# First stage of a two-block network on one NeuronCore: the input rows requested first, the first quarter of the modulation as TensorE matmuls

## The chip, the cores and the metric

One core of a Trainium2 chip runs one program. The metric is the device time of a run in microseconds. The engines that matter are TensorE (PE in the profile, its weight loads PEld), VectorE (DVE), ScalarE (ACT) and the queue on SyncE (SP) that issues every load from memory.

## The reference, cut to what matters

Two blocks, each of depth 2, work on 256 rows of 1024 features. The program's first stage is the opening of the first block's first layer:

```python
cond = jax.nn.silu(c)                       # c: (1, 1024)
mod = cond @ ada_w[l] + ada_b[l]            # ada_w[l]: (1024, 9 * 1024)
sh1, sc1, g1, ... = jnp.split(mod, 9, axis=-1)
hn = _modulate(_rms_norm(h, norm_g[l, 0]), sh1, sc1)   # xn * (1 + scale) + shift
h = h + 0.5 * g1[:, None, :] * _swiglu(hn, ffn1_w_in[l], ffn1_w_out[l])
```

Before the first feed-forward product can begin, the rows of x have to be normed, turned to feature-major form, scaled by `(1 + sc1) * norm_g` and shifted by `sh1`. Scale and shift are products of the vector `cond` with 1024 x 1024 pieces of `ada_w`.

## The kernel before, in words

Every large product runs as three float32r matmuls: operands are split into a high part (`A.copy` with a cast, line 336, ACT) and the rest (`V.tensor_tensor` subtract, line 339, DVE), and `mm3` (lines 368 to 370) adds high x high, high x low and low x high. Weights come as parts of 128 x 1024 floats (512 KB): `load_part` (line 345) takes a raw buffer `wr`, a high buffer `wh` and a low buffer `wl`, and issues the load on SP (line 347). There are three `wr` buffers; one is free again when both halves of the split have read it. A part serves 12 matmuls of 128 x 512: two blocks of 128 features, two row tiles, three products.

The modulation is done on VectorE. `ada_load` (line 678) brings 128 output columns of `ada_w`, laid out one per partition with 1024 inputs along it, and `ada_chunk` (line 683) multiplies them with `cond`, which stands as a copy in every partition, and sums along the partition: one value per partition, a column of `mod`.

`start()` (line 723) is the first stage. It computes the first four of the eleven feed-forward column groups (`FIRST`), and goes through the 1024 features in four pairs of blocks (`p` = 0 to 3, blocks k = 2p and 2p+1). Each pair needs four chunks of the modulation (scale and shift of its two blocks) and four weight parts, and then issues 48 matmuls. Ahead of the pairs stands the row work: `row_rstd` sums squares (line 476, ACT) and takes the reciprocal root (lines 442 to 447), line 740 scales the rows, line 489 transposes them on TensorE against the identity `ident`, which is part of the table `col_sb`, and line 743 copies the result to `xts`. `modulate(k)` (line 747) makes scale and shift out of the two columns of `mod`, applies them on ACT (line 753), casts to `xh` (line 754) and subtracts to `xl` (line 755).

The program is written in the order of the work, and a scheduler of the framework sets each engine's own instruction order at build time. On the chip every engine runs its list strictly in order, and so does SP: a load that waits for a buffer holds up all loads behind it.

```python
for p, pair in enumerate(pairs):
    ...
    for j in range(2):
        for n in pair[2 * j:2 * j + 2]:
            if p or n[1]:
                ada_chunk(0, sum(n), raws.pop(n))
        modulate(2 * p + j)
        for n in range(2 * j, FIRST if j else 2):
            raw, hi, lo = parts[n]
            split(hi, lo, raw)
```

Of the kernel before, what the change touches and what calls it, by code (L numbers as in the profile page):

```python
# [9 lines left out]
F32 = mybir.dt.float32  # L10
F32R = mybir.dt.float32r
BF16 = mybir.dt.bfloat16
# [11 lines left out]
FIRST = 4  # L24
# [156 lines left out]


def pack(inp):
    d = {"ws": pack_weights(inp), "cols": pack_cols(inp), "x": inp["x"].reshape(S, D), "c": inp["c"].reshape(1, D)}
    aw = inp["ada_w"]
    d["adaw"] = aw.reshape(2, D, 72, 128).transpose(0, 2, 3, 1)
    wf = inp["w_in"][:, :, 2560:2564]
    d["wf"] = wf.reshape(2, 8, 128, 4).transpose(2, 0, 1, 3)
    d["gmn"] = np.stack([inp["gmlp_norm_g"], inp["gmlp_norm_b"]], 1).reshape(1, 1024)
    d["wst"] = inp["gmlp_ws"].transpose(3, 0, 1, 2)  # L190
    import ml_dtypes

    def level(b):
        j, t = np.arange(128)[:, None], np.arange(128)[None, :]
        mid = t // (2 * b) * 2 * b + b
        return np.where(t >= mid, (j >= mid) & (j <= t), (j > t) & (j < mid)).astype(np.float32)
# [23 lines left out]
INS = ["ws", "cols", "x", "c", "adaw", "wf", "gmn", "wst", "bmask", "lev", "pred", "sbias", "gains", "lbs"]  # L220


@with_exitstack
def body(ctx, tc, ws, cols, x, c, adaw, wf, gmn, wst, bmask, lev, pred, sbias, gains, lbs, out, phases=range(12)):
    nc = tc.nc
    V, A, T = nc.vector, nc.scalar, nc.tensor
    phases = list(phases)
# [21 lines left out]
    def s2(shape=(128, 512), dt=F32):  # L249
        return s2_p.tile(list(shape), dt, tag="s2", name=nm("s"))  # L250
# [232 lines left out]
    def hh(t, q):  # L483
        return h[:, t, 512 * q:512 * q + 512]
# [183 lines left out]
    const.tile([128, 8], F32, name="trail")  # L668
# [53 lines left out]

    def start():

        pairs = [[(o, k) for k in (2 * p, 2 * p + 1) for o in (8, 0)] for p in range(4)]
# [9 lines left out]
        xts = [s2([128, 2, S]) for _ in range(4)]  # L735
# [8 lines left out]
        acc = [[accum(), accum()] for _ in range(FIRST)]  # L744
        w = [{} for _ in range(FIRST)]

        def modulate(k):
            an_, mod_ = an[0][:, k:k + 1], mod[0][:, k:k + 1]
            A.activation(an_, mod[0][:, 8 + k:9 + k], AF.Identity, scale=C("norm_g", k, 1), bias=g1[:, k:k + 1])
            A.activation(mod_, mod_, AF.Identity, bias=C("ada_b", k, 1))  # L750
# [4 lines left out]
            V.tensor_tensor(out=xl[:, k], in0=xt, in1=xh[:, k].bitcast(F32), op=ALU.subtract)  # L755

        for p, pair in enumerate(pairs):
            half, i = divmod(p, 2)
            parts = []
            for n in pair:  # L760
                if p or n[1]:
                    raws[n] = ada_load(0, sum(n))
            for n in range(FIRST):
                parts.append(load_part(plan["b1", 0, "ffn1", n, half], i))
            for j in range(2):
                for n in pair[2 * j:2 * j + 2]:
                    if p or n[1]:
                        ada_chunk(0, sum(n), raws.pop(n))
# [731 lines left out]
```

## Time and profile before

| | us |
|---|---|
| median of 3 runs | 2214.31 |
| lowest and highest run | 2205.01, 2215.36 |
| the profiled execution | 2208.89 |
| its span in the profile | 2207.1 |
| TensorE busy | 2149.9 (97%) |
| VectorE busy | 1486.1 (67%) |
| ScalarE busy | 1191.5 (54%) |
| loads of 512 KB: weight parts, modulation chunks | 692, 144 |

The profile shows one execution. "Busy" adds the time in which an engine has an instruction under way; matmuls overlap in the pipeline, so the distance between the starts of two of them is less than the duration printed for one. Where a row has "xN" the times are of N instructions merged. A true float32 matmul (not float32r, not a transpose) stands in the trace as two pairs of weight load and matmul: line 944 issues 48 of them in the program, and the trace has 96.

### The profile page before, as it was taken

Reading aid. Unit: us, or ns where it says so; the run is one execution under the profiler, and the core shown is the slowest. Engines: PE = TensorE matmul, PEld = TensorE weight load, DVE = VectorE, ACT = ScalarE, POOL = GpSimd, SP = SyncE. Lnnn points to the kernel's source line nnn. Section 1 sums busy time; section 2 is a strip of 40 time slices with the busy share of each in tenths; the row PEclk is TensorE's granted clock in tenths of the full one; section 3 lists DMA queues with packets and bytes.
Section 4 is the critical chain, followed back from the end, with each engine's and each line's share of the span. In section 5 each row is a group of like instructions: output and inputs, shape, how many; then the busy total and the mean of one; then the engine's idle time right before and its main releaser. Section 6 shows DMA issues by size and latency. Waiting matters only on the chain.

```text
span 2207.1 us, 27771 instructions
## 1 busy us (share of the span) xinstructions
PE 2149.9 (97%) x10148; PEld 1765.8 (80%) x10150; DVE 1486.1 (67%) x2224; ACT 1191.5 (54%) x1933; POOL 0.2 (0%) x4
## 2 busy tenths in 40 slices
PE   6999998999999999999999999999999999999998
PEld 5787776888888777888888888888888887887887
DVE  6788986765888786655754665675566557657653
ACT  6544656544544756553644565464465447556552
POOL 0000000000000000000000000000000000000000
PEclk9999998999999999999999999999999999999999
DMA  8889734885889533755755543475555555245652
GB/s 321 294 318 337 259 118 152 293 265 174 314 336 342 209 113 126 247 181 183 246 187 188 179 143 115 135 234 184 191 181 202 189 171 183 96 143 177 205 182 95
DMA packets 125416, 452.90 MB, mean 205 GB/s; under 512 B 14176, under 2 KB 14432, under 8 KB 125280
## 3 DMA queue, kind: packets, MB, share of 16 engines
q1 hardware_dynamic: 125280, 451.13, 59.2%
q8 instruction: 80, 1.31, 0.2%
q14 instruction: 56, 0.46, 0.1%
HBM read 450.03 MB, written 1.05 MB: 204 GB/s over the span
## 4 chain that ended last, share of the span: by engine, by line
PE 77%; DMA 8%; ACT 7%; DVE 6%; issue 2%; SPq 0%; DVEq 0%; ACTq 0%
PE a L368 23%; PE a L369 22%; PE a L370 22%; DMA wr<-in_ws 8%; ACT wh L336 3%; DVE wl L339 3%; PE t L626 2%; PE t L489 1%; PE t L1234 1%; ACT h L476 1%; DVE spill L683 1%; ACT s L533 1%; PE t L1188 1%; PE t L970 1%; PE t L1346 0%
## 5 line engine op out<-in xcount | busy, mean ns | idle before, releaser
L339 DVE TENSOR_TENSOR wl<-wr,wh 128x1024 fp32r<-128x1024 f32 x692 | 843.2, 1223 | 468.0 <-ACT wh L336 463.0
L336 ACT CAST wh<-wr 128x1024 fp32r<-128x1024 f32 x692 | 726.8, 1052 | 718.5 <-PE a L370 388.1
L368 PE MATMUL a<-wh,xh 128*128 128x512 f32 x1888 | 750.7, 398 | 7.9 <-ACT xh L534 6.0
L369 PE MATMUL a<-wl,xh 128*128 128x512 f32 x1888 | 736.4, 390 | 1.9 <-DVE wl L339 1.9
L370 PE MATMUL a<-wh,xl 128*128 128x512 f32 x1888 | 736.0, 391 | 0.0
L368 PEld LDWEIGHTS a<-wh,xh 128*128 128x128 f32 x1888 | 357.6, 189 | 81.6 <-ACT xh L534 6.7
L370 PEld LDWEIGHTS a<-wh,xl 128*128 128x128 f32 x1888 | 356.9, 189 | 75.5 <-DVE xl L339 1.4
L369 PEld LDWEIGHTS a<-wl,xh 128*128 128x128 f32 x1888 | 357.6, 189 | 73.0 <-DVE wl L339 3.7
L368 PE MATMUL a<-wh,s 128*128 128x512 f32 x896 | 352.2, 393 | 3.9 <-ACT s L336 2.8
L369 PE MATMUL a<-wl,s 128*128 128x512 f32 x896 | 350.8, 392 | 0.8 <-DVE wl L339 0.8
L370 PE MATMUL a<-wh,s 128*128 128x512 f32 x896 | 349.3, 391 | 0.0
L368 PEld LDWEIGHTS a<-wh,s 128*128 128x128 f32 x896 | 168.9, 188 | 39.8 <-ACT s L336 3.4
L369 PEld LDWEIGHTS a<-wl,s 128*128 128x128 f32 x896 | 168.9, 188 | 35.6 <-DVE wl L339 1.6
L370 PEld LDWEIGHTS a<-wh,s 128*128 128x128 f32 x896 | 168.7, 188 | 35.3 <-DVE s L339 0.6
L683 DVE CUSTOM_DVE_ANT_0 spill<-ada,cond 128x1024 bf16<-128x1024 f32 x144 | 175.5, 1219 | 5.9 <-DMA ada<-in_adaw 5.3
L489 PE MATMUL t<-col_sb,s 128*128 128x128 f32 x304 | 45.9, 285 | 27.3 <-ACT s L740 18.3
L489 PEld LDWEIGHTS t<-col_sb,s 128*128 128x128 f32 x304 | 35.1, 144 | 41.7 <-ACT s L740 19.1
L339 DVE TENSOR_TENSOR s<-t,s 128x512 fp32r<-128x512 f32 x96 | 64.9, 684 | 3.4 <-ACT s L336 3.4
L626 PE MATMUL t<-col_sb,h 128*128 128x128 f32 x392 | 58.9, 274 | 6.2 <-DVE h L594 3.2
L626 PEld LDWEIGHTS t<-col_sb,h 128*128 128x128 f32 x392 | 48.0, 141 | 19.6 <-DVE h L594 4.3
L590 ACT ACTIVATE h<-a,m 128x256 f32<-128x256 f32 x88 | 40.7, 473 | 36.4 <-PE a L370 36.3
L336 ACT CAST s<-t 128x512 fp32r<-128x512 f32 x96 | 54.9, 582 | 5.6 <-PE t L626 5.6
(241 smaller groups left out, 1251.5 us busy)
## 6 DMA issues: line engine op xcount, KB each, us to landing
wr<-in_ws SPq DMA_DIRECT2D x692, 512.0 KB, 4.0
ada<-in_adaw SPq DMA_DIRECT2D x144, 512.0 KB, 5.7
row<-in_gains SPq DMA_DIRECT2D x12, 512.0 KB, 4.9
h<-in_x SPq DMA_DIRECT2D x2, 512.0 KB, 7.3
out<-h SPq DMA_DIRECT2D x4, 256.0 KB, 2.0
cond<-in_c SPq DMA_DIRECT2D x1, 512.0 KB, 4.3
gmn<-in_gmn SPq DMA_DIRECT2D x2, 256.0 KB, 5.1
wst<-in_wst SPq DMA_DIRECT2D x2, 256.0 KB, 6.2
```

What stands on the lines that cost most here:

```text
L336: ins = A.copy(dst_h, src)
L339: return V.tensor_tensor(out=dst_l, in0=src, in1=dst_h.bitcast(F32), op=ALU.subtract)
L368: T.matmul(acc, a, wh, start=start, stop=False)
L369: T.matmul(acc, a, wl, start=False, stop=False)
L370: T.matmul(acc, b, wh, start=False, stop=stop)
L476: A.activation(junk, src, AF.Square, accum_out=ss[:, i:i + 1])
L489: T.transpose(ps[:, j], src[:, 128 * j:128 * j + 128], ident)
L533: A.activation(xt[:, j], ps[:, j], AF.Identity, scale=a, bias=b)
L590: A.activation(g, acc[t][:, 0:256], AF.Silu, scale=r)
L626: T.transpose(ps[:, i, 128 * t:128 * t + 128], src[t][:, 128 * i:128 * i + 128], ident)
L683: ins = V.tensor_tensor_reduce(out=spill, in0=raw, in1=cond, scale=1.0, scalar=0.0, op0=ALU.mult, op1=ALU.add, accum_out=mod[l][:, n:n + 1])
L970: T.matmul(ps[:, i], qT[rs, i, ts], kT[rs, i, 0:keys], start=False, stop=i == 1)
```

## The change

The row tiles of x and the table `col_sb` are requested ahead of any modulation chunk. The vector c comes as a 128 x 8 tile (`scc`, 4 KB) with one feature per partition. The four chunks of the first pair are laid out anew on the host (`adaf`, inputs on the partitions) and are multiplied on TensorE: eight 128 x 128 weight loads with a moving operand of one column each, added up in one column of a PSUM tile (`pm`). The other 140 chunks stay on VectorE, and the spread copy `cond` that they need is made on the chip by eight transposes of `scc` and two copies. Of the row work, half of the squares, of the scalings and of the copies out of PSUM goes from ACT to DVE. For the first pair, the making of scale and shift also goes to DVE. The casts of the first four weight parts now stand behind the row work in ACT's list. Sizes and all later stages are unchanged.

```diff
@@ def pack
+    "cc": inp["c"].reshape(8, 128).T
+    first = aw[0, :, :2 * D].reshape(8, 128, 2, 8, 128)[:, :, :, :2]
+    d["adaf"] = first.transpose(3, 2, 1, 0, 4).reshape(2, 2, 128, D)
@@ def start
-        raws = {n: ada_load(0, sum(n)) for n in pairs[0][:2]}
         for t in range(2):
             nc.sync.dma_start(out=h[:, t], in_=x[128 * t:128 * t + 128])
         nc.sync.dma_start(out=col_sb, in_=cols)
-        for n in pairs[0][:2]:
-            ada_chunk(0, sum(n), raws.pop(n))
+        for o, k in pairs[0]:
+            raw = ada_p.tile([128, D], F32, tag="ada", name=nm("ada"))
+            nc.sync.dma_start(out=raw, in_=adaf[k, 1 if o else 0])
+            raws[o, k] = raw
+        xts = [s2([128, 2, S]) for _ in range(4)]
+        for t in range(2):
+            A.activation(junk, hh(t, 0), AF.Square, accum_out=ss[:, 0:1])
+            V.tensor_tensor_reduce(out=junk, in0=hh(t, 1), in1=hh(t, 1), scale=1.0, scalar=0.0, op0=ALU.mult,
+                                   op1=ALU.add, accum_out=ss[:, 1:2])
+            V.tensor_tensor(out=r, in0=ss[:, 0:1], in1=ss[:, 1:2], op=ALU.add)
+            rsqrt(r, r, 1.0 / D)
+            A.activation(xss[t][0], hh(t, 0), AF.Copy, scale=r)
+            V.tensor_scalar(out=xss[t][1], in0=hh(t, 1), scalar1=r, scalar2=None, op0=ALU.mult)
...
-        for t in range(2):
-            r = row_rstd([hh(t, 0), hh(t, 1)])
-            for q in range(2):
-                xs = s2()
-                A.activation(xs, hh(t, q), AF.Copy, scale=r)
-                ps = transposed(xs)
-                for i in range(2):
-                    A.copy(xts[2 * q + i][:, :, 128 * t:128 * t + 128], ps[:, 2 * i:2 * i + 2])
+        pm = tp([128, 4])
+        for n, key in enumerate(pairs[0]):
+            raw = raws.pop(key)
+            for kb in range(8):
+                T.matmul(pm[:, n:n + 1], raw[:, 128 * kb:128 * kb + 128], scc[:, kb:kb + 1], start=kb == 0,
+                         stop=kb == 7)
+            if n < 2:
+                features(n, 0)
+        parts0 = [load_part(plan["b1", 0, "ffn1", n, 0], 0) for n in range(FIRST)]
+        def rest_of_start():
+            for t in range(2):
+                features(t, 1)
+            for q in range(2):
+                ps = tp([128, 4, 128])
+                for j in range(4):
+                    T.transpose(ps[:, j], scc[:, 4 * q + j:4 * q + j + 1].to_broadcast([128, 128]), ident)
+                A.copy(cond[:, 512 * q:512 * q + 512], ps.rearrange("p a b -> p (a b)"))
         def modulate(k):
+            if k < 2:
+                V.scalar_tensor_tensor(out=an_, in0=pm[:, 2 * k:2 * k + 1], scalar=C("norm_g", k, 1),
+                                       in1=g1[:, k:k + 1], op0=ALU.mult, op1=ALU.add)
+                V.tensor_tensor(out=mod_, in0=pm[:, 2 * k + 1:2 * k + 2], in1=C("ada_b", k, 1), op=ALU.add)
...
+            if p == 0:
+                rest_of_start()
+                acc = [[accum(), accum()] for _ in range(FIRST)]
@@ body
-        nc.sync.dma_start(out=cond, in_=c.to_broadcast([128, D]))
-        A.activation(cond, cond, AF.Silu)
+        scc = const.tile([128, 8], F32, name="scc")
+        nc.sync.dma_start(out=scc, in_=cc)
+        A.activation(scc, scc, AF.Silu)
```

How the lists move is seen at three places. First TensorE, from the program's start to the first product of the feed-forward layer (`a_...` is its accumulator, `s_137` to `s_181` scaled rows, `t_...` PSUM tiles, `t_162` the new `pm`). Before:

```order
L489 MATMUL t_139<-col_sb,s_137 128x128 x4
L489 MATMUL t_148<-col_sb,s_146 128x128 x4
L489 MATMUL t_172<-col_sb,s_170 128x128 x4
L489 MATMUL t_181<-col_sb,s_179 128x128 x4
L368 MATMUL a_188<-wh_202,xh 128x512
```

With the change (line numbers are those of the changed program):

```order
L765 MATMUL t_162<-scc,ada_110 128x1 x8
L491 MATMUL t_171<-col_sb,s_137 128x128 x4
L491 MATMUL t_186<-col_sb,s_156 128x128 x3
L765 MATMUL t_162<-scc,ada_112 128x1 x8
L491 MATMUL t_186<-col_sb,s_156 128x128
L491 MATMUL t_243<-col_sb,s_138 128x128 x4
L491 MATMUL t_250<-col_sb,s_157 128x128
L765 MATMUL t_162<-scc,ada_114 128x1 x8
L491 MATMUL t_250<-col_sb,s_157 128x128 x3
L777 MATMUL t_257<-col_sb,scc 128x128 x4
L777 MATMUL t_263<-col_sb,scc 128x128 x4
L765 MATMUL t_162<-scc,ada_116 128x1 x8
L370 MATMUL a_269<-wh_211,xh 128x512
```

The four groups of eight one-column matmuls stand between the transposes, the last of them behind the eight transposes that make `cond`, and the first product stands behind all of it.

Then ScalarE, from the scaling of the rows to the first casts of weight parts (`wh<-wr`). Before:

```order
L740 ACTIVATE s_137<-h,m_127 128x512
L442 ACTIVATE m_163<-m_160,epsc 128x1
L443 ACTIVATE m_163<-m_163 128x1
L336 CAST wh_202<-wr_200 128x1024
L743 COPY s_118<-t_139 128x2x128
L743 COPY s_119<-t_139 128x2x128
L740 ACTIVATE s_146<-h,m_127 128x512
L336 CAST wh_206<-wr_204 128x1024
```

With the change:

```order
L760 COPY s_118<-t_186 128x2x128
L760 COPY s_119<-t_186 128x2x128
L778 COPY cond<-t_257 128x512
L778 COPY cond<-t_263 128x512
L792 ACTIVATE s_118<-s_118,mod_91,an_93 128x256 x2
L793 CAST xh<-s_118 128x256
L338 CAST wh_211<-wr_209 128x1024
L793 CAST xh<-s_118 128x256
L338 CAST wh_215<-wr_213 128x1024
L338 CAST wh_219<-wr_217 128x1024
L338 CAST wh_223<-wr_221 128x1024
```

Before, the first two casts stand in the midst of the row work; now the first stands behind the application of scale and shift (line 792) and the first cast of `xh` (line 793).

Last SP, from its first load on. Before:

```order
L1420 DMA cond<-in_c 128x1024
L678 DMA ada_107<-in_adaw 128x1024
L678 DMA ada_109<-in_adaw 128x1024
L728 DMA h<-in_x 128x1024 x2
L729 DMA col_sb<-in_cols 128x880
L678 DMA ada_196<-in_adaw 128x1024
L678 DMA ada_198<-in_adaw 128x1024
L347 DMA wr_200<-in_ws 128x1024
L347 DMA wr_204<-in_ws 128x1024
L347 DMA wr_208<-in_ws 128x1024
L678 DMA ada_284<-in_adaw 128x1024
L347 DMA wr_212<-in_ws 128x1024
```

With the change:

```order
L1464 DMA scc<-in_cc 128x8
L727 DMA h<-in_x 128x1024 x2
L728 DMA col_sb<-in_cols 128x880
L733 DMA ada_110<-in_adaf 128x1024
L733 DMA ada_112<-in_adaf 128x1024
L733 DMA ada_114<-in_adaf 128x1024
L733 DMA ada_116<-in_adaf 128x1024
L349 DMA wr_209<-in_ws 128x1024
L349 DMA wr_213<-in_ws 128x1024
L349 DMA wr_217<-in_ws 128x1024
L679 DMA ada_325<-in_adaw 128x1024
L349 DMA wr_221<-in_ws 128x1024
```

The rows and the table move ahead of the chunks; the fourth weight part stays the twelfth load, behind one chunk of the second pair, and waits as before for a free `wr` buffer.

## Rows read from the trace of the kernel before

**Rows 1.** The page: busy us of each engine, share of the span, instructions.

```profile
PE 2149.9 (97%) x10148; PEld 1765.8 (80%) x10150; DVE 1486.1 (67%) x2224; ACT 1191.5 (54%) x1933; POOL 0.2 (0%) x4
```

**Rows 2.** Busy time by stretch: us from start, length, engines, PEclk, DMA share, GB/s.

```profile
0.00:10.00 10.00, 0.00 (x0) 0.00 (x0) 3.36 (x8) 3.62 (x3) 0.20 (x4) 1.00 0.82 292
10.00:20.00 10.00, 2.23 (x8) 1.43 (x8) 4.40 (x19) 8.27 (x23) 0.00 (x0) 1.00 0.90 358
24.30:60.00 35.70, 35.42 (x148) 28.89 (x149) 26.94 (x38) 20.87 (x35) 0.00 (x0) 1.00 0.83 308
100.00:140.00 40.00, 40.00 (x186) 33.12 (x185) 34.83 (x53) 16.96 (x23) 0.00 (x0) 1.00 0.90 318
```

**Rows 3.** The chain of waits, 0 to 90 us: start, us, what.

```profile
3.16 8.17 DMA col_sb<-in_cols
50.11 6.77 DMA wr<-in_ws
```

**Rows 4.** The timeline, loads and their first users: start us, us, engine, instruction [idle before].

```profile
0.73 0.39 SPq L1420 DMA_DIRECT2D cond<-in_c  x1
5.08 1.06 ACT L1421 ACTIVATE cond<-cond 128x1024 f32<-128x1024 f32 x1 [3.08 <-DMA cond<-in_c]
18.15 0.33 SPq L347 DMA_DIRECT2D wr<-in_ws  x1
```

**Rows 5.** The weight parts' buffers (wr), 0 to 60 us: issue to landing.

```profile
DMA to landing us min/median/max: 3.2/6.2/10.0
```

**Rows 6.** The timeline: the row work on ACT and DVE.

```profile
6.59 1.23 DVE L683 CUSTOM_DVE_ANT_0 spill<-ada,cond 128x1024 bf16<-128x1024 f32 x1 [4.82 <-DMA ada<-in_adaw]
11.63 0.61 ACT L476 ACTIVATE h<-h 128x512 bf16<-128x512 f32 x1
13.17 0.29 ACT L442 ACTIVATE m<-m,epsc 128x1 f32<-128x1 f32 x1
14.59 0.16 DVE L447 SCALAR_TENSOR_TENSOR m<-m,m 128x1 f32<-128x1 f32 x1
14.79 0.72 ACT L740 ACTIVATE s<-h,m 128x512 f32<-128x512 f32 x1
```

**Rows 7.** The timeline of TensorE: eight transposes early and late, and first products.

```profile
20.55 1.97 PE L489 MATMUL t<-col_sb,s 128*128 128x128 f32 x8 [1.36 <-ACT s L740]
24.32 0.79 PE L368 MATMUL a<-wh,xh 128*128 128x512 f32 x1 [1.80 <-ACT xh L754]
24.91 0.63 PE L369 MATMUL a<-wl,xh 128*128 128x512 f32 x1
219.02 1.07 PE L489 MATMUL t<-col_sb,s 128*128 128x128 f32 x8 [0.56 <-DVE s L512]
```

**Rows 8.** True float32 matmuls: timeline, and weight loads by line (busy, mean ns).

```profile
301.78 2.79 PE L944 MATMUL t<-s,s 128*128 128x64 f32 x24
...
L944 PEld LDWEIGHTS t<-s,s 128*128 128x128 f32 x96 | 11.3, 192 | 0.3
L1212 PEld LDWEIGHTS t<-s 128*32 128x32 f32 x64 | 2.3, 108 | 1.9
```

**Rows 9.** Busy time of a stretch at the lower granted clock.

```profile
222.30:225.60 3.30, 3.30 (x9) 2.54 (x9) 2.37 (x4) 3.30 (x9) 0.00 (x0) 0.50 1.02 397
```

**Rows 10.** The timeline: splits of weight parts, and scale and shift applied.

```profile
15.83 1.03 ACT L336 CAST wh<-wr 128x1024 fp32r<-128x1024 f32 x1
16.89 1.23 DVE L339 TENSOR_TENSOR wl<-wr,wh 128x1024 fp32r<-128x1024 f32 x1 [0.39 <-ACT wh L336]
23.09 0.61 ACT L753 ACTIVATE s<-s,mod,an 128x256 f32<-128x256 f32 x1
23.59 0.38 ACT L749 ACTIVATE an<-mod,m,col_sb 128x1 f32<-128x1 f32 x1
23.87 0.40 ACT L754 CAST xh<-s 128x256 fp32r<-128x256 f32 x1
24.30 0.42 DVE L755 TENSOR_TENSOR xl<-s,xh 128x256 fp32r<-128x256 f32 x1 [0.54 <-ACT xh L754]
```

More of the change, by code (lines that the diff above doesn't have):

```diff
@@ L183, in pack @@
 def pack(inp):
-    d = {"ws": pack_weights(inp), "cols": pack_cols(inp), "x": inp["x"].reshape(S, D), "c": inp["c"].reshape(1, D)}
+    d = {"ws": pack_weights(inp), "cols": pack_cols(inp), "x": inp["x"].reshape(S, D), "cc": inp["c"].reshape(8, 128).T}
     aw = inp["ada_w"]
+    first = aw[0, :, :2 * D].reshape(8, 128, 2, 8, 128)[:, :, :, :2]
+    d["adaf"] = first.transpose(3, 2, 1, 0, 4).reshape(2, 2, 128, D)
     d["adaw"] = aw.reshape(2, D, 72, 128).transpose(0, 2, 3, 1)
@@ L217, in pack, with body @@
     return {k: np.ascontiguousarray(v) for k, v in d.items()}
-INS = ["ws", "cols", "x", "c", "adaw", "wf", "gmn", "wst", "bmask", "lev", "pred", "sbias", "gains", "lbs"]
+INS = ["ws", "cols", "x", "cc", "adaf", "adaw", "wf", "gmn", "wst", "bmask", "lev", "pred", "sbias", "gains", "lbs"]
 @with_exitstack
-def body(ctx, tc, ws, cols, x, c, adaw, wf, gmn, wst, bmask, lev, pred, sbias, gains, lbs, out, phases=range(12)):
+def body(ctx, tc, ws, cols, x, cc, adaf, adaw, wf, gmn, wst, bmask, lev, pred, sbias, gains, lbs, out, phases=range(12)):
     nc = tc.nc
@@ L667, in body @@
     an = [const.tile([128, 24], F32, name=f"an{l}") for l in range(2)]
-    const.tile([128, 8], F32, name="trail")
     c1 = pool("c1", 1, first_block)
@@ L723, in start @@
     def start():
-        pairs = [[(o, k) for k in (2 * p, 2 * p + 1) for o in (8, 0)] for p in range(4)]
-        raws = {n: ada_load(0, sum(n)) for n in pairs[0][:2]}
         for t in range(2):
@@ L729, in start @@
         nc.sync.dma_start(out=col_sb, in_=cols)
-        for n in pairs[0][:2]:
-            ada_chunk(0, sum(n), raws.pop(n))
+        pairs = [[(o, k) for k in (2 * p, 2 * p + 1) for o in (8, 0)] for p in range(4)]
+        raws = {}
+        for o, k in pairs[0]:
[3 more added lines that the diff above has]
+        xts = [s2([128, 2, S]) for _ in range(4)]
+        xss = []
+        for t in range(2):
+            ss, r = sm(2), sm(1)
+            junk = s1([128, 512], BF16)
+            A.activation(junk, hh(t, 0), AF.Square, accum_out=ss[:, 0:1])
+            junk = s1([128, 512], BF16)
+            V.tensor_tensor_reduce(out=junk, in0=hh(t, 1), in1=hh(t, 1), scale=1.0, scalar=0.0, op0=ALU.mult,
+                                   op1=ALU.add, accum_out=ss[:, 1:2])
+            V.tensor_tensor(out=r, in0=ss[:, 0:1], in1=ss[:, 1:2], op=ALU.add)
+            rsqrt(r, r, 1.0 / D)
+            xss.append((s2(), s2()))
+            A.activation(xss[t][0], hh(t, 0), AF.Copy, scale=r)
+            V.tensor_scalar(out=xss[t][1], in0=hh(t, 1), scalar1=r, scalar2=None, op0=ALU.mult)
         g1 = sm(8)
@@ L734, in start, with features @@
                                op1=ALU.mult)
-        xts = [s2([128, 2, S]) for _ in range(4)]
-        for t in range(2):
-            r = row_rstd([hh(t, 0), hh(t, 1)])
-            for q in range(2):
-                xs = s2()
-                A.activation(xs, hh(t, q), AF.Copy, scale=r)
-                ps = transposed(xs)
-                for i in range(2):
-                    A.copy(xts[2 * q + i][:, :, 128 * t:128 * t + 128], ps[:, 2 * i:2 * i + 2])
-        acc = [[accum(), accum()] for _ in range(FIRST)]
+        def features(t, q):
+            ps = transposed(xss[t][q])
+            for i in range(2):
+                dst = xts[2 * q + i][:, :, 128 * t:128 * t + 128]
+                if q:
+                    V.tensor_copy(out=dst, in_=ps[:, 2 * i:2 * i + 2])
+                else:
+                    A.copy(dst, ps[:, 2 * i:2 * i + 2])
+        pm = tp([128, 4])
[10 more added lines that the diff above has]
+                features(t, 1)
+            for q in range(2):
+                ps = tp([128, 4, 128])
+                for j in range(4):
+                    T.transpose(ps[:, j], scc[:, 4 * q + j:4 * q + j + 1].to_broadcast([128, 128]), ident)
+                A.copy(cond[:, 512 * q:512 * q + 512], ps.rearrange("p a b -> p (a b)"))
         w = [{} for _ in range(FIRST)]
@@ L748, in modulate @@
             an_, mod_ = an[0][:, k:k + 1], mod[0][:, k:k + 1]
-            A.activation(an_, mod[0][:, 8 + k:9 + k], AF.Identity, scale=C("norm_g", k, 1), bias=g1[:, k:k + 1])
-            A.activation(mod_, mod_, AF.Identity, bias=C("ada_b", k, 1))
+            if k < 2:
+                V.scalar_tensor_tensor(out=an_, in0=pm[:, 2 * k:2 * k + 1], scalar=C("norm_g", k, 1),
+                                       in1=g1[:, k:k + 1], op0=ALU.mult, op1=ALU.add)
+                V.tensor_tensor(out=mod_, in0=pm[:, 2 * k + 1:2 * k + 2], in1=C("ada_b", k, 1), op=ALU.add)
+            else:
+                A.activation(an_, mod[0][:, 8 + k:9 + k], AF.Identity, scale=C("norm_g", k, 1), bias=g1[:, k:k + 1])
+                A.activation(mod_, mod_, AF.Identity, bias=C("ada_b", k, 1))
             known.update(((0, k), (0, 8 + k)))
@@ L755, in modulate @@
             V.tensor_tensor(out=xl[:, k], in0=xt, in1=xh[:, k].bitcast(F32), op=ALU.subtract)
+        acc = None
         for p, pair in enumerate(pairs):
@@ L759, in start @@
             parts = []
-            for n in pair:
-                if p or n[1]:
+            if p:
+                for n in pair:
                     raws[n] = ada_load(0, sum(n))
-            for n in range(FIRST):
-                parts.append(load_part(plan["b1", 0, "ffn1", n, half], i))
+                parts = [load_part(plan["b1", 0, "ffn1", n, half], i) for n in range(FIRST)]
+            else:
+                parts = parts0
             for j in range(2):
-                for n in pair[2 * j:2 * j + 2]:
-                    if p or n[1]:
-                        ada_chunk(0, sum(n), raws.pop(n))
+                for n in pair[2 * j:2 * j + 2] if p else []:
+                    ada_chunk(0, sum(n), raws.pop(n))
                 modulate(2 * p + j)
```

## The prediction, made before the changed kernel ran

> **What bounds the kernel now.** I read the page first: TensorE is busy 97% of the span [rows 1], so a change must take work from it, fill a hole in it, or open one. Then the busy time by stretch: the large hole is the start. TensorE has nothing in the first 10 us and 2.23 us in the next ten, while the load engines move 292 and then 358 GB/s; from 24.3 on it is full: 35.42 of 35.70 us, and 40.00 of 40.00 later [rows 2]. So only the time of the first product, 24.32 us [rows 7], is at stake, and whether the weights keep up behind it.
>
> The chain of waits tells how near they are to not keeping up. In the first 90 us it does not run along TensorE but through loads: the table `col_sb`, issued at 3.16, is on it for 8.17 us, and later a weight part for 6.77 us [rows 3]. The reader should see two lines of supply in the first stage: the one that gets the normed, modulated rows ready, and the loop of three raw buffers (load, cast, subtract, next load). Before, the loop is early: its first cast starts at 15.83 and its first subtract at 16.89 [rows 10], and the fourth weight part is requested at 18.15 [rows 4], 6.2 us ahead of the first product.
>
> **Part by part.** All times are us from the span's start.
>
> Loads. Before, the spread `cond` lands at about 5.08, 4.35 after its issue [rows 4], and `col_sb` at 3.16 + 8.17 = 11.33 [rows 3]; between them lie two chunks, two row tiles and the 440 KB of the table, so 6.25 us for 2,488 KB: 1.29 per 512 KB. Now 4 KB go first, then the rows. The first row tile is issued about 0.44 later than `cond` was and lands 3.2 [rows 5] to 4.35 after that, 4.4 to 5.5; I take 5.0. The second tile follows at 6.3, the table at 7.4, the chunks at 8.7, 10.0, 11.3 and 12.6. Rows and table thus come some 4 us sooner than now.
>
> Row work. Per tile: squares of both halves side by side (0.61 and about half of 1.23), some small steps of 0.16 to 0.29, the scaling at 0.72 [rows 6]. The first scaled half is ready near 9.2, the last near 10.7, against 20.5 for the last transposes before. Nine microseconds are gained here if nothing else stands in the way.
>
> TensorE's new work stands in the way. Its list begins with the eight one-column matmuls of the first chunk, at 8.7 at the earliest, and ends with those of the fourth; between them stand 16 transposes of rows and 8 that make `cond`. The trace has no one-column matmul. It has true float32 matmuls of 64 columns, which count as two pairs of weight load and product; 24 such pairs take 2.79 late in the run, 0.116 each [rows 8]. A narrower product need not help: a load of 32 columns of weights takes 108 ns, one of 128 takes 192 [rows 8], so 96 columns cost 84 ns and 128 some 0.11, the whole price of the pair. That is at the full clock. Early on, eight transposes take 1.97 where they take 1.07 later [rows 7], and at the granted clock of 0.50 (1.2 GHz) 9 matmuls fill 3.30 us [rows 9], against 0.215 each in a full stretch (40.00 us, 186 of them) [rows 2]. So at the lower level a pair costs 0.116 x 1.97 / 1.07 = 0.214. The 32 matmuls are 64 pairs, 13.7; the 24 transposes at 0.246 are 5.9; together 19.6. No later input breaks this line: the chunks land faster than they are used up. It ends at 8.7 + 19.6 = 28.3. Bounds of the pair: 0.06 (half the full-clock price) and 0.25 (an early transpose); I take 0.214, because the same weights are loaded in rows 8.
>
> From there to the first product: two small steps on DVE, 0.3; scale and shift on ACT, which starts the next instruction 0.50 after the first, twice 0.5; a cast of 0.40; and then the first weight part's cast, 1.03 [rows 6, 10], which now stands behind all this. First product at 28.3 + 0.3 + 1.0 + 0.4 + 1.03 = 31.0, **6.7 later than now**.
>
> The row steps moved to DVE, the spread of `cond` on chip and the four products less on DVE (4 x 1.31) I cost at nothing: they lie beside TensorE's line of 19.6 us. Were that line short, the row work would end it near 11 and they would count for at most about 2.
>
> Supply behind the first product, M. The first subtract ends at M + 1.2; only then is the fourth part requested (before: M - 6.2). It lands at M + 4.5, its low half is ready at M + 6.8, when TensorE is just through the other three. Behind it in SP's list stand three chunks of the second pair, so the fifth part lands at M + 4.5 + 4 x 1.29 = M + 9.7, with its halves at M + 12.0; the first 48 matmuls, some of them at the lower clock, end at about M + 12. The eighth part is requested only when the fifth has freed its buffer, M + 12, lands at M + 15.2 and is ready at M + 17.5, where TensorE wants it at M + 16. DVE has 4 subtracts, 4 chunk products and 2 short subtracts per pair, 4 x 1.23 + 4 x 1.31 + 2 x 0.42 = 11.0, against 48 x 0.215 = 10.3 of TensorE, so the lead that before was built up while TensorE was idle cannot be built up now. I put 1 us on each of the three further pairs, 3; ends: 0, as the trace of before has hardly any wait there [rows 2], and 4.8, the 1.6 us three times. Nothing later gives it back: TensorE is full for the next 40 us and more [rows 2].
>
> Sum: +6.7 + 3 = +9.7. The profiled execution took 2208.89, its span is 1.8 less; that makes 2218.6. It lies 5.4 below the median of the runs shown, 2214.31; the four executions known (2205.01, 2208.89, 2214.31, 2215.36) have a mean of 2210.9, and with 9.7 on that I name **2221**.
>
> **The rivals.** 0.5% is 11 us, about what a measurement of this kernel can tell from no change.
>
> (a) The clock rises under the small matmuls. If it goes up near 15.5, 31 of the 88 steps are done by then and the other 57 take 0.11 each: end at 22, first product at 24.7, and that product starts at the full clock, which saves 8 x (0.37 - 0.215) = 1.2. With 3 to 4 for supply the sum is +2 to +4, about 2212 on the profiled execution. For it: TensorE would have no gap from 8.7 on. Against it: the 16 transposes that end at 22.5 did not raise it before; the first products still took 0.63 [rows 7] as under the lower clock. The Trainium skill (TensorE: Matmul & The Clock Gate, Part 1: The HAM clock gate) says that the rate follows how busy the engine has been and not how many instructions it ran; by that rule an unbroken stream is enough, and this rival is the one that comes. No row of this trace shows a stream of weight loads with next to no columns behind them.
>
> (b) Not slower: a one-column pair costs little. At 0.06 the 64 pairs are 3.8, the line ends near 8.7 + 3.8 + 5.9 = 18.4, the first product stands at 21.1, 3.2 early, and supply gives back 0 to 4: 2206 to 2210. It decides where a pair at the lower clock costs 0.06 (with 3 for supply; 0.11 with none) or less. For it: the product itself is a column wide. Against it: the 192 ns of the loads [rows 8].
>
> (c) Slower by over 0.5%: the buffer loop. If each of the three further pairs loses the 1.6 us, and a pair costs 0.23, the sum is 7.7 + 4.8 = +12.5, 2221 on the profiled execution, 2227 on the median.
>
> **How the numbers follow.** The forecast (clock low, +8 to +11) 0.57; (a) 0.18; (b) 0.11; (c) 0.14. The range runs from (a) and part of (b) on the profiled execution, 2209, to (c) on the median with a little more, 2229. More than 11 us faster would need the first product near 13, before the fourth chunk has landed: 0.05, for what I have not seen. Slower by over 0.5%: (c), the upper edge of the forecast and the spread of the runs, 0.31. Within: 0.64.
>
> **What would show it.** Right: one-column matmuls from about 8.7, some 3.5 us for each chunk, two pairs each; the first product near 31 at the lower clock; the chain of waits along TensorE up to 28 and through casts and weight parts after it; waits of TensorE on `wl` or `wh` between 40 and 75; later stages shifted as a whole. Wrong: a first product before 25, a pair well under 0.2, or a clock at its upper level before 20.

## The result: a ratio of 1.0069, first product at 30.12

The changed kernel took 2226.56 us (median of 7 runs), the kernel before 2209.36 in 7 runs beside them: a ratio of 1.0069, 95% interval 1.0051 to 1.0087, some 15 us (11 to 19). The time lies in the predicted range, 5.6 above the forecast of 2221; the loss itself was forecast at 9.7 us. The whole interval is above 0.5%, to which the prediction gave 0.31.

The profiled execution took 2233.02, its span is 2231.2. The page's engine line, which answers to [rows 1]:

```profile
PE 2169.7 (97%) x10222; PEld 1780.3 (80%) x10222; DVE 1484.5 (67%) x2230; ACT 1187.9 (53%) x1921; POOL 0.2 (0%) x4
```

The shares say nothing: TensorE is as full as before, of a longer span. Busy time by stretch does; the second, third and fourth rows are the stretches of [rows 2], the others are new (columns as there):

```profile
8.73:27.30 18.57, 18.57 (x88) 18.50 (x88) 2.29 (x8) 3.29 (x8) 0.00 (x0) 1.00 0.44 178
10.00:20.00 10.00, 10.00 (x49) 10.00 (x50) 0.76 (x2) 1.30 (x4) 0.00 (x0) 1.00 0.68 278
24.30:60.00 35.70, 31.04 (x124) 24.09 (x124) 22.77 (x34) 18.58 (x29) 0.00 (x0) 1.00 0.68 251
100.00:140.00 40.00, 40.00 (x184) 32.98 (x184) 35.38 (x54) 16.25 (x23) 0.00 (x0) 1.00 0.90 308
20.00:30.00 10.00, 7.31 (x35) 7.23 (x35) 1.66 (x7) 3.44 (x7) 0.00 (x0) 1.00 0.00 0
```

Three things are to be seen. The new line of 88 steps (64 pairs and 24 transposes) holds TensorE without a gap from 8.73 to 27.30. From 24.30 to 60.00 TensorE has 31.04 busy microseconds of 35.70, where it had 35.42; the first product now stands inside that stretch. And in the last row the load engines move nothing at all for ten microseconds; up to 27.30 TensorE works on the modulation. The column PEclk gives 1.00 in all of them, but its first record in this trace stands at 34.30; until then the level has to be read from durations.

TensorE's timeline up to the first product, answering to [rows 7] (start, us, engine, line, tiles; a row of x16 is one chunk):

```profile
8.73 3.54 PE L765 MATMUL t<-scc,ada 128*128 128x1 f32 x16 [8.73 <-DMA ada<-in_adaf]
12.14 1.73 PE L491 MATMUL t<-col_sb,s 128*128 128x128 f32 x7
13.66 3.41 PE L765 MATMUL t<-scc,ada 128*128 128x1 f32 x16
16.94 1.52 PE L491 MATMUL t<-col_sb,s 128*128 128x128 f32 x6
18.25 3.41 PE L765 MATMUL t<-scc,ada 128*128 128x1 f32 x16
21.52 0.88 PE L491 MATMUL t<-col_sb,s 128*128 128x128 f32 x3
22.20 1.91 PE L777 MATMUL t<-col_sb,scc 128*128 128x128 f32 x8
23.90 3.41 PE L765 MATMUL t<-scc,ada 128*128 128x1 f32 x16
30.12 1.22 PE L370 MATMUL a<-wh,xh 128*128 128x512 f32 x2 [2.81 <-ACT wh L338]
31.98 0.63 PE L372 MATMUL a<-wh,xl 128*128 128x512 f32 x1
34.43 0.40 PE L371 MATMUL a<-wl,xh 128*128 128x512 f32 x1
```

Each chunk takes 3.41, two pairs to a matmul as [rows 8] let expect; the products still take 0.63 at 31.98 and 0.40 only from 34.43, so the clock was at its lower level (1.2 GHz) through all of the line. Then the timeline of ACT, DVE and the queue, answering to [rows 10] and the last row of [rows 4]:

```profile
27.35 0.22 DVE L784 SCALAR_TENSOR_TENSOR an<-t,col_sb,m 128x1 f32<-128x1 f32 x1 [4.16 <-PE t L765]
27.74 1.09 ACT L792 ACTIVATE s<-s,mod,an 128x256 f32<-128x256 f32 x2 [3.00 <-DVE mod L786]
29.03 1.04 ACT L338 CAST wh<-wr 128x1024 fp32r<-128x1024 f32 x1
30.10 1.23 DVE L341 TENSOR_TENSOR wl<-wr,wh 128x1024 fp32r<-128x1024 f32 x1 [0.52 <-ACT wh L338]
31.35 0.33 SPq L349 DMA_DIRECT2D wr<-in_ws  x1
```

The first split begins at 29.03 instead of 15.83, and the fourth weight part is requested at 31.35 instead of 18.15. What that does to TensorE is in its waits, 24 to 100 us (us in total, times, longest):

```profile
PE a L370 <- ACT wh L338: 4.4, 3, 2.8
PE a L371 <- DVE wl L341: 3.0, 6, 0.8
```

The longest, 2.8, is the one ahead of the first product. In the kernel before, the same stretch has this one wait for weights:

```profile
PE a L369 <- DVE wl L339: 1.1, 3, 0.5
```

The chain of waits, answering to [rows 3], runs along TensorE's line and then through loads and splits:

```profile
24.11 3.22 PE t L765 x16
29.12 0.95 ACT wh L338
31.58 2.37 DVE wl L341 x2
33.96 8.53 DMA wr<-in_ws
48.70 6.21 DMA wr<-in_ws
57.27 4.04 DMA wr<-in_ws
```

Where the time went is plainest in when the pairs of blocks begin (the products of the first layer counted in the trace, 48 to a pair): before at 24.3, 36.9, 47.8, 58.7, and the next stage at 71.8; now at 30.1, 43.3, 56.2, 71.5 and 85.6. So 5.8 us were lost ahead of the first product and 8.0 more in the four pairs. The rest of the profile's loss of 24.1 came later, most of it between 640 and 760 us and near 1270 us; a second profile, below, does not have it.

### The profile page after: what moved, and what is told of

It is laid out like the page before. It is cut to its first block, busy times and chain, and to the rows that moved or that the text cites. A ratio compares the mean times of both kernels' runs of the same rounds, so it can differ in the third digit from the quotient of the medians.

```text
span 2231.2 us, 27911 instructions
## 1 busy us (share of the span) xinstructions
PE 2169.7 (97%) x10222; PEld 1780.3 (80%) x10222; DVE 1484.5 (67%) x2230; ACT 1187.9 (53%) x1921; POOL 0.2 (0%) x4
## 4 chain that ended last, share of the span: by engine, by line
PE 67%; DMA 14%; DVE 8%; ACT 7%; issue 3%; SPq 0%; ACTq 0%; DVEq 0%
PE a L370 19%; PE a L372 19%; PE a L371 19%; DMA wr<-in_ws 13%; DVE wl L341 4%; ACT wh L338 4%; PE t L628 2%; DVE spill L684 1%; PE t L491 1%; PE t L1277 1%; ACT s L535 1%; PE t L1231 1%; ACT h L478 1%; PE t L765 1%; PE t L1013 1%
## 5 line engine op out<-in xcount | busy, mean ns | idle before, releaser
L370 PE MATMUL a<-wh,xh 128*128 128x512 f32 x1888 | 749.5, 399 | 12.6 <-ACT xh L536 6.0
L684 DVE CUSTOM_DVE_ANT_0 spill<-ada,cond 128x1024 bf16<-128x1024 f32 x140 | 170.7, 1219 | 3.5 <-DMA ada<-in_adaw 2.8
L628 PE MATMUL t<-col_sb,h 128*128 128x128 f32 x392 | 59.7, 275 | 7.1 <-DVE h L596 3.2
L592 ACT ACTIVATE h<-a,m 128x256 f32<-128x256 f32 x88 | 40.7, 473 | 37.0 <-PE a L372 36.9
L653 ACT ACTIVATE s<-t,m 128x128 f32<-128x128 f32 (+1 forms) x80 | 32.8, 418 | 46.7 <-DVE m L651 26.6
```

What stands on the lines that cost most here:

```text
L370: T.matmul(acc, a, wh, start=start, stop=False)
L592: A.activation(g, acc[t][:, 0:256], AF.Silu, scale=r)
L628: T.transpose(ps[:, i, 128 * t:128 * t + 128], src[t][:, 128 * i:128 * i + 128], ident)
L653: uses(A.activation(pb[:, i], ps[:, i], AF.Exp, bias=nmx[:, i:i + 1], accum_out=sums[:, cols[i]:cols[i] + 1]))
L684: ins = V.tensor_tensor_reduce(out=spill, in0=raw, in1=cond, scale=1.0, scalar=0.0, op0=ALU.mult, op1=ALU.add, accum_out=mod[l][:, n:n + 1])
```

## The experiments

Two losses were suspected, a late first product (TensorE's new line) and splits that begin late and leave the loads no lead. All times are us; "last pair" is the start of the fourth pair of blocks. A high product is one of high part by high part (`a<-wh,xh`), 16 to a pair; the 72nd, and below the 240th of all products, are counted from 0 and lie behind the four pairs. The ratio is to the kernel before, with its 95% interval. The lines without an interval were run once; every start of a stage is that of one profiled execution.

| run | first split | first product | last pair | 72nd high product | ratio |
|---|---|---|---|---|---|
| before | 15.83 | 24.32 | 58.7 | 78.3 | |
| changed kernel | 29.03 | 30.12 | 71.5 | 92.2 | 1.0069 (1.0051 to 1.0087) |
| after_again | 29.04 | 30.13 | 69.3 | 89.7 | |
| casts_early | 18.48 | 29.70 | 65.0 | 85.1 | 1.0011 (0.9999 to 1.0023) |
| half_products | 22.11 | 23.20 | 64.0 | 84.5 | 1.0031 (1.0017 to 1.0045) |
| half_and_casts | 14.72 | 24.38 | 59.7 | 77.7 | 0.9984 (0.9969 to 0.9998) |
| rows_first_vector | 17.00 | 18.09 | 58.9 | 79.7 | 0.9998 (0.9979 to 1.0018) |
| vector_casts_early | 14.25 | 16.30 | 58.3 | 76.9 | 1.0000 (0.9987 to 1.0014) |
| dense_first | 20.31 | 21.40 | 60.1 | 80.2 | |
| dense_casts_early | 14.53 | 21.27 | 57.0 | 76.7 | 1.0008 (0.9994 to 1.0022) |
| rows_on_act | 27.55 | 28.64 | 69.3 | 90.1 | |
| before_casts_late | 23.42 | 24.55 | 65.5 | 85.7 | 1.0031 (1.0015 to 1.0048) |
| no_chunks | 28.95 | 30.04 | 64.8 | 82.1 | |

**casts_early: the splits ahead of the modulation.** `after(x, y)` orders x behind y in an engine's list. The edit also holds some copies of the row work and of `cond` behind the splits, and the second pair's chunk products behind the modulation.

```diff
+        for n in range(4):
+            raw, hi, lo = parts0[n]
+            subs.append(split(hi, lo, raw, firsts.append))
+            w[n].setdefault(0, []).append((hi, lo))
...
-            A.activation(xt, xt, AF.Identity, scale=an_, bias=mod_)
+            ins = A.activation(xt, xt, AF.Identity, scale=an_, bias=mod_)
+            if k == 0:
+                after(ins, firsts[-1])
```

> The changed kernel, with the splits of the first four weight parts put ahead of the modulation of block 0 in the lists of ScalarE and VectorE; nothing else differs. Theory (the start lost 5.8 us by the modulation on TensorE, and some 8 us because the splits of the first weight parts stand behind it, so that the fourth part is requested at 31.35 instead of 18.15): the first product comes one cast earlier, at 29.1 (28.6 to 30); the fourth part is requested before 18; the 72nd high product comes 54 to 56 us after the first as before the change (54.0), at 83 to 86 instead of 92.2; the time is 7 to 9 us under that of the changed kernel. Rival (the loss behind the first product is that of the loads and of the clock, whatever the order of the splits): first product at 29.1, the 72nd at 90 to 91, and 1 us gained.

The first product came at 29.70, the 72nd high product at 85.1: the theory's numbers. The fourth part was requested at 20.82, not before 18, since the splits stood behind a copy out of PSUM that waited for TensorE's line until 17.95. The waits of TensorE for weights are gone, 24 to 100 us:

```profile
PE a L370 <- ACT xh L799: 4.3, 2, 2.4
PE t L628 <- DVE h L596: 0.7, 1, 0.7
```

The first product moved by 0.4, the last pair by 6.5, so the second loss comes from where the splits stand. The gain on the changed kernel is 7.1 us by the 72nd high product, as expected; against its second profile (after_again) it is 4.6, and the last pair moved by 4.3. By the ratios the gain is 13 (1.0069 less 1.0011), more than expected, but the two are known to 4 and 3 us.

**half_products: half of TensorE's new work.** Half of the sum of the first four chunks is left out.

```diff
-            for kb in range(8):
+            for kb in range(4):
```

> The changed kernel with four instead of eight one-column matmuls per chunk: half of the sum of the first four chunks is left out, 32 pairs of weight load and product less; the order of the splits is as in the changed kernel. Theory (a pair costs 0.214 us on TensorE's line at the lower clock): first product 32 x 0.214 = 6.8 us earlier, at 23.3; the supply loss of about 8 us behind it stays, so the 72nd high product comes at 23.3 + 54 + 8 = 85, and the time is 6 to 8 us under that of the changed kernel. Rival 1 (a pair is cheap and the line is set by the transposes and the row work): first product 2 us earlier, 28, and 2 us gained. Rival 2 (the supply loss comes from the first product being late): first product at 23.3, the 72nd at 78, and 13 to 15 us gained.

First product at 23.20, 6.92 earlier: 0.216 us for each of the 32 pairs that were left out, and the stage behind it as slow as in the changed kernel (last pair 40.8 behind the first product, there 41.4). A cheap pair and a loss that would go with the late first product are both refuted: the first product stands 1.1 ahead of the kernel before, and the ratio is still 1.0031.

**half_and_casts: both edits.**

> Both edits together: four instead of eight one-column matmuls per chunk (half of the sum of the first four chunks is left out) and the first four splits ahead of the modulation. Theory (two separate losses that add up): first product at 22.3, the 72nd high product at 76 to 78, before the change 78.3; the time is that of the kernel before, or 2 us under it, and 14 to 17 us under the changed kernel. Rival (losses that cover each other): no more than the larger of the two single gains, 8 to 9 us under the changed kernel.

The 72nd high product came at 77.7, 14.5 ahead of the changed kernel where the two single gains (7.1 and 7.6) make 14.7: the two losses add up. The ratio is 0.9984, some 3.5 us (0.4 to 7) under the kernel before, where up to 2 were expected; but half of the sum is left out here. The first product was missed, at 24.38 for 22.3. The timeline of ACT says why: the fourth split, ahead of the modulation in this run, waits for its load, and the modulation with it.

```profile
20.34 1.04 ACT L338 CAST wh<-wr 128x1024 fp32r<-128x1024 f32 x1 [0.56 <-DMA wr<-in_ws]
22.94 1.09 ACT L796 ACTIVATE s<-s,mod,an 128x256 f32<-128x256 f32 x2 [1.55 <-DVE mod L790]
```

**rows_first_vector: the modulation back on VectorE, rows first.**

```diff
-            for kb in range(8):
-                T.matmul(pm[:, n:n + 1], raw[:, 128 * kb:128 * kb + 128], scc[:, kb:kb + 1], ...)
+        for n, key in enumerate(pairs[0]):
+            ada_chunk(0, sum(key), raws.pop(key))
...
-                    T.transpose(ps[:, j], scc[:, 4 * q + j:4 * q + j + 1].to_broadcast([128, 128]), ident)
+        nc.sync.dma_start(out=cond, in_=c.to_broadcast([128, D]))
```

> The changed kernel with the modulation of the first quarter back on VectorE: the spread copy of c is loaded first again, then rows, table and the four chunks in the layout of before; no one-column matmuls, no transposes for the spread copy; the row work stays shared, and the splits stay behind the modulation. Theory (TensorE's new work is what delays the first product; rows first and shared row work are sound): first product at 16.5 (15.5 to 18), 8 us sooner than before; the loads then set the pace, a pair of blocks needs 8 loads of 1.29 us, so part of this is given back; the 72nd high product comes at 72 to 76 (before 78.3), and the time is 2 to 6 us under that of the kernel before. Rival (the supply loss of 8 us follows from the splits behind the modulation wherever the modulation is done): first product at 16.5, the 72nd at 78 to 79, and the time of before.

Here the rival came. The first product stood at 18.09, 6.2 us ahead of the kernel before, and all of it was lost again by the last pair, 58.9 against 58.7; the time is that of before. Rows first and shared row work do what they are meant to. They do not pay here. That this is because the splits begin no earlier (17.00, before 15.83) is not shown, as the next run tells.

**vector_casts_early: the same with earlier splits.** The first weight parts are requested between the chunks and split at once.

```diff
         for o, k in pairs[0]:
             raws[o, k] = ada_load(0, o + k)
+            if k or not o:
+                parts0.append(load_part(plan["b1", 0, "ffn1", len(parts0), 0], 0))
...
+            if n == 2:
+                after(ins, subs[0])
```

> The run rows_first_vector (modulation of the first quarter on VectorE, rows and table first, shared row work) with three changes of order: weight parts 1 and 2 are requested between the chunks, each split is made as soon as its part is there, ahead of the modulation, and the small row steps stand ahead of the first chunk product. Theory (both losses were separate: TensorE's line, and splits behind the modulation): first product at 15 to 17; the fourth part is requested near 15 instead of 19.77; no load gap before 25, so the 16th part lands near 8.8 + 32 x 1.29 = 50 and the last pair begins at 53 to 56 (before 58.7, rows_first_vector 58.9); the 72nd high product at 73 to 75 (before 78.3); the time 3 to 5 us under that of the kernel before. Rival (the four pairs cannot go faster than loads and VectorE let them, some 11 us a pair from the first landing, whatever the order): first product at 16, the last pair at 58 to 59 and the time of before.

The rival again: the first product at 16.30, 8 us early, the last pair at 58.3. The first split, 2.75 ahead of that of rows_first_vector and 1.6 ahead of the kernel before, moved the last pair by about half a microsecond. The 16th part landed at 61.06, not at 50. TensorE waits for the weights and for the rows of each pair in turn, 16 to 75 us:

```profile
PE a L369 <- DVE wl L339: 2.8, 5, 0.8
PE a L368 <- ACT xh L795: 2.5, 3, 1.0
PE a L370 <- DVE xl L796: 0.6, 1, 0.6
```

From the runs up to here, with dense_first and rows_on_act below, a rule could be read, good to some 2 us: the last pair begins at the later of the first product + 35 (TensorE's own pace) and the first split + 42 (the pace of the supply). vector_casts_early fits it worst but for dense_first: 58.3, where the rule has 56.3. Two more runs, dense_casts_early and before_casts_late, were made to test it.

**dense_first and dense_casts_early: the clock.** TensorE gets 22 products of 128x512 bf16 on zeros while it would be idle; the second run has casts_early's edit as well, for three parts.

```diff
+        wz = s2([128, 512], BF16)
+        V.memset(wz, 0.0)
+        dz = tp([128, 512])
+        for i in range(22):
+            T.matmul(dz, wz[:, 0:128], wz, start=True, stop=True)
```

> The changed kernel with 22 products of 128x512 bf16 on a zeroed tile ahead of the one-column matmuls, in the stretch in which TensorE has no input; their result is not used. Theory A (the stream of one-column matmuls neither raises the clock nor holds it): the dense products bring the clock up near 6, it falls again while the chunks are multiplied, the later chunks take 3.4 us each again, first product at 26 to 30. Rival B (the stream does not raise the clock but holds it): all four chunks take about 1.9 us each (pair 0.116), first product at 21 to 24, and it runs at the upper level from the start. Rival C (the dense block does not raise the clock either): chunks at 3.4 us, the line pushed back, first product at 31 to 34.

TensorE's timeline of dense_first, and its busy time from the first one-column matmul to the last and behind the first product (the clock's first record stands at 6.17 in this trace):

```profile
1.24 7.34 PE L730 MATMUL t<-s 128*128 128x512 bf16 x22 [1.24 <-DVE s L727]
8.79 1.92 PE L770 MATMUL t<-scc,ada 128*128 128x1 f32 x16 [0.21 <-DMA ada<-in_adaf]
11.92 1.84 PE L770 MATMUL t<-scc,ada 128*128 128x1 f32 x16
14.97 3.63 PE L770 MATMUL t<-scc,ada 128*128 128x1 f32 x32
21.40 1.22 PE L370 MATMUL a<-wh,xh 128*128 128x512 f32 x2 [2.81 <-ACT wh L338]
23.25 0.63 PE L372 MATMUL a<-wh,xl 128*128 128x512 f32 x1
```

```profile
8.79:18.60 9.81, 9.80 (x88) 9.72 (x88) 2.28 (x8) 3.09 (x8) 0.00 (x0) 1.00 0.82 334
21.00:26.00 5.00, 4.56 (x10) 3.19 (x11) 4.62 (x5) 2.55 (x4) 0.00 (x0) 0.50 0.48 160
```

The same 88 steps take 9.81 us here and 18.57 in the changed kernel. B holds in its first part: this stream of one-column matmuls and transposes did not let the upper level (2.4 GHz) go in its 9.81 us. Its last part failed: behind 2.8 us without work the first products stand at 0.63 again, with a granted clock of 0.50 from 21.00 to 26.00, the lower level. The clock costs this kernel 8.7 us ahead of the first product.

> The changed kernel with 22 products of 128x512 bf16 on a zeroed tile ahead of the one-column matmuls (their result is not used) and with the first three splits ahead of the modulation. Theory (first split near 14.5, first product near 20.3, so that 14.5 + 42 and 20.3 + 35.3 both give 56 to 57): last pair at 55.5 to 58 (before 58.7), the time 1 to 3 us under that of the kernel before, which is not to be told from it. Rival (the upper clock of the run dense_first was that execution's luck): chunks at 3.4 us again, first product at 25 to 30, the time 2 to 6 us over.

The clock repeated itself (chunks of 1.92, 1.84 and 3.63 for two), and the last pair came at 57.0, where the rule has 56.5 and 56.3. The start gained 1.6 us by the 72nd high product; the whole run cannot be told from the kernel before (1.0008).

**rows_on_act: is the row work covered?**

```diff
-            V.tensor_tensor_reduce(out=junk, in0=hh(t, 1), in1=hh(t, 1), ...)
+            A.activation(junk, hh(t, 1), AF.Square, accum_out=ss[:, 1:2])
...
-            V.tensor_scalar(out=xss[t][1], in0=hh(t, 1), scalar1=r, scalar2=None, op0=ALU.mult)
+            A.activation(xss[t][1], hh(t, 1), AF.Copy, scale=r)
```

> The changed kernel with the shared row work put back on ScalarE (second squares, second scaling, second half of the copies out of PSUM). Theory (TensorE's line of 19.6 us covers the row work, as the prediction put it): first product at 29.5 to 30.8 as in the changed kernel (30.12), one-column matmuls from 8.7. Rival (the sharing is what makes the rows ready in time): the transposes break TensorE's line, first product at 32 or later.

No transpose breaks TensorE's line, and the first product came at 28.64, earlier than the range, not later. The row work is covered. The gain is not its doing: the fourth chunk took less in this execution, behind twelve transposes nearly in a row, and four of the transposes for `cond` stand behind it:

```profile
21.05 1.95 PE L491 MATMUL t<-col_sb,s 128*128 128x128 f32 x8
22.79 1.06 PE L773 MATMUL t<-col_sb,scc 128*128 128x128 f32 x4
23.64 2.19 PE L761 MATMUL t<-scc,ada 128*128 128x1 f32 x16
25.70 0.63 PE L773 MATMUL t<-col_sb,scc 128*128 128x128 f32 x4
```

Here the clock did rise within the line, some 15 us after its start at 9.32: four transposes take 1.06 at 22.79 and 0.63 at 25.70, and the clock's first record stands at 24.36.

**before_casts_late: one part of the change alone, in the kernel before.** The edit shown puts the splits behind the modulation; five small loads of later stages are held back as well, so that they stay where they were.

```diff
-                    split(hi, lo, raw)
+                    split(hi, lo, raw, None if p else lambda ins: after(ins, xhs[0]))
```

> The kernel before with one part of the change alone: the splits of the first weight parts are kept behind the modulation of block 0 (loads, modulation and row work as before; five small loads of later stages are held behind the loads of the start, so that they stay where they were). Theory (the start's last pair of blocks begins at the later of two times: first product + 35, or first split + 42, as in the runs so far, where late splits gave 39.8 to 42.5): first split near 24.2, first product 25.3, last pair at 64 to 67 (before 58.7), the time 5 to 8 us over that of the kernel before, a ratio of 1.002 to 1.004. Rival (late splits only cost the one cast that moves onto the path): first product 25.3, last pair at 60, the time 1 us over.

First split 23.42, last pair 65.5, 42.1 behind it, ratio 1.0031: the rule's number, and half of the change's loss without any of its new work. (The first product came at 24.55, as the row work in ACT's list ended sooner without the casts in its midst.)

**no_chunks: what the supply is made of.**

```diff
-                for n in pair:
-                    raws[n] = ada_load(0, sum(n))
...
-                for n in pair[2 * j:2 * j + 2] if p else []:
-                    ada_chunk(0, sum(n), raws.pop(n))
```

> The changed kernel without the 12 modulation chunks of the second to fourth pair: their loads and their products on VectorE are left out, scale and shift of blocks 2 to 7 are made from zeros. Splits stay behind the modulation. Theory (the supply line that the late splits begin is made of 28 loads and the work of VectorE on them; with 16 loads TensorE sets the pace): first product at 30.1, last pair at 65 to 66.5, first product + 35 to 36 (changed kernel: 71.53). Rival (the three raw buffers alone hold it: load, cast, subtract, next load): last pair at 69 to 72.

Last pair at 64.8, 0.2 under the range, 34.8 behind the first product. Groups of TensorE by line between 28 and 72 us, of the changed kernel and then of this run (busy, mean ns | idle before, releaser):

```profile
L371 PE MATMUL a<-wl,xh 128*128 128x512 f32 x48 | 19.6, 412 | 1.5 <-DVE wl L341 1.5
L370 PE MATMUL a<-wh,xh 128*128 128x512 f32 x49 | 18.6, 426 | 5.5 <-ACT wh L338 4.4 <-ACT xh L793 1.1
```

```profile
L371 PE MATMUL a<-wl,xh 128*128 128x512 f32 x59 | 23.5, 400 | 0.0
L370 PE MATMUL a<-wh,xh 128*128 128x512 f32 x59 | 23.1, 406 | 2.7 <-ACT wh L338 2.7
```

With late splits and three raw buffers, but without the twelve chunks and their products, TensorE waits for one cast, its first, and never again. So it is weight parts and chunks together that run slower than TensorE, not the buffers alone. Whether the chunks count by their loads or by their products on VectorE is not separated. (Behind the stage this run loses again, 8.8 us behind the kernel before at its 240th product; that was not followed up.)

**after_again: is the later loss the change's?**

> The changed kernel once more, for a second profile. Theory (what the first profile lost behind 240 us, 10.5 us in steps near 760, 1140 and 1300 us, belongs to that execution and not to the change): first product at 30.1, last pair at 70.5 to 72.5, the 240th of the first layer's products near 100, and from there to the end 2117 to 2125 us (before 2120.6), so a span of 2217 to 2225. Rival (later stages lose by the change too): the same steps at the same places, a span of 2229 to 2233.

First product at 30.13, last pair at 69.3, 1.2 us under the range, and the 240th product at 97.1, where near 100 was expected (before 86.5). From there to the end it took 2119.8, before 2120.6, with a span of 2216.9. The steps of the first profile did not come again. Up to the 240th product the change cost 13.6 us in one profile and 10.6 in the other.

## Why the prediction was right, and where it was not

**The line of TensorE: right, 1.0 too long.** Predicted 19.6 us from 8.7 to 28.3, measured 18.57 from 8.73 to 27.30. The pair came near the 0.214 of the text (0.204 to 0.213 a pair from a chunk's start to the next instruction's, 0.216 by half_products). The transposes were taken at 0.246 and stand 0.217 apart (seven start within 1.52): a group's duration contains the end of its last instruction.

**From there to the first product: right.** 2.73 predicted, 2.82 measured, in the order of the text: scale and shift, cast of the rows, cast of the first part. First product at 30.12 for 31.0.

**The supply: the mechanism was right, the size was not.** Fourth part requested at first product + 1.2 and landing at + 4.5: measured 31.35 and 34.67, to the tenth. But "I put 1 us on each of the three further pairs, 3", with an upper end of 4.8, is the step that failed. Measured over all four pairs were 8.0, and 5.6 in the second profile. Of this the first pair has 0.6 and 1.2; it took 13.2 and 13.8 where the text has some 12 (before: 12.6). The three further pairs lost 7.4 and 4.4 where the text has 3. The step looked for the wait of one part, the eighth, and compared VectorE's 11.0 us a pair with TensorE's 10.3. The runs show it in another way. In the seven runs whose splits come late (no_chunks left out) the last pair begins 39.8 to 42.5 us behind the first split; where the splits have a lead of 6.7 us or more, or no chunks are to be loaded, TensorE needs 34.4 to 35.7 from its first product. The supply thus needs some 7 us more than TensorE (42 less 35). Before, the first split was 8.5 us ahead of the first product, which covers this; now it is 1.1 ahead, so some 6 are lost. What the first profile lost beyond that has late landings in it (the chain's 8.53 and 6.21), but these were not separated. The lead should have been priced as a lead: 42 less 35 less 1.1, or 5.9. One run stands outside: vector_casts_early, with a lead of 2.0, begins its last pair 44.1 behind its first split. Why its supply was slower stays open.

**The time in the range: in part luck.** The first product came 0.9 early and the pairs lost more than forecast, so the sum of 9.7 stands against 13.6 and 10.6 in the two profiles and 15 (11 to 19) in the ratio. The upper end of the range, 2229, was (c)'s 12.5 on the median of three runs, 2214.31, with a little more; on the 2209.36 measured beside the changed kernel the same 12.5 gives 2221.9, under the 2226.56 that came.

**Row work, and the moves to DVE, at nothing: right** (rows_on_act). **Nothing gives it back: right** (after_again keeps the 10.6 to within a microsecond up to the end, 9.8).

**The rivals.** (a), the rising clock, did not come in either profile of the changed kernel. The Trainium skill (TensorE: Matmul & The Clock Gate, Part 1: The HAM clock gate) has the rate follow how busy the engine has been; by that an unbroken stream should have raised it. The trace disagrees for the 18.57 us of this one, agrees in rows_on_act, where it rose at 24.36, and in dense_first, where the level held for 9.81 us. What tells the cases apart was not tried. (b), a cheap pair, is refuted by half_products. (c) came nearest in size: 12.5 predicted, 13.6 and 10.6 in the profiles; its price of a pair, 0.23, was not needed, as the four pairs lost 8.0 and 5.6 against its 4.8.

## What to carry to other kernels

An engine's idle time at the start is not free if other engines stock up in it: count by how much the first split, load or cast runs ahead of the first product, and what the pace of the supply is against that of the consumer, before moving work ahead of it in a list. This stage ends with the later of two lines, within some 2 us: a first product that came 6.2 us sooner (rows_first_vector) or 8.0 (vector_casts_early) moved its end by less than one. No version here that does all of the work beats the kernel before by what can be measured; the best start, dense_casts_early, is 1.6 us ahead at the 72nd high product.

## What was not expected of the hardware

A pair with one moving column takes about as long as a transpose with 128: 0.21 us at the lower level (transposes stand 0.217 apart), 0.11 at the upper (9.81 us for 88 steps). TensorE was busy without a gap for 18.57 us at the lower level, and with 7.3 us of dense products ahead it did the same work at the upper level throughout. The column PEclk showed 1.00 in a stretch of which the durations show the lower level: where the trace has no record yet, durations are the evidence.
